# FFN output product of an encoder trunk: three pieces of Strassen's scheme and four tiles in the old form, in place of the direct product

## The chip, the cores and the metric

The kernel runs on one core of one Trainium2 chip, in one launch. The metric is the time of an execution in microseconds on the device; lower is better. Five engines of the core matter here: TensorE (PE; its weight loads are listed as PEld), VectorE (DVE), ScalarE (ACT), GpSimd (POOL) and SyncE (SP), which issues the transfers.

## The reference

Four post-norm layers over x of 512 tokens by 1024 features in float32. The mixers of the layers are multi-head latent attention, retention, gated linear attention and latent attention again. After each mixer comes a dense FFN with 2816 hidden features, and both are added to alpha times x and normalised:

```python
def swiglu_ffn(x, w_in, w_out):
    gate, up = jnp.split(x @ w_in, 2, axis=-1)
    return (jax.nn.silu(gate) * up) @ w_out
# in each layer, twice:  x <- layer_norm(alpha * x + sublayer(x))
```

The change touches the last product alone: 512 x 2816 by 2816 x 1024, once in each of four layers.

## The kernel before

Every float32 product is made of three matmuls on operands that are split into a rounded part hi and a rest lo: hi by hi, hi by lo, lo by hi (`mm3`, L126 to L130). ScalarE makes hi by a cast (L102), VectorE makes lo by a subtraction (L103). Weights arrive by transfers from SP's queue into one of three raw buffers (`wraw`), and their parts go to one of six `whi` and six `wlo` (`wload` and `wsplit`, L106 to L121). For six weights after the end of each stage POOL makes lo instead of VectorE (`relieve`). Sums stand in six buffers of PSUM (`ps`); two more (`tp`) take transposes.

The x of the layer is held twice: `xt`, four token tiles of 128 x 1024 in float32, which the layers add to and normalise, and `xh`, `xl`, its transposed and split form.

The FFN (`ffn`, L298) goes over 22 tiles of 128 hidden features. The first three are computed in two halves of the tokens, while the end of the mixer's normalisation still runs. Each later one takes a gate and an up projection of 24 matmuls of 512 columns each. `evac` then applies silu on ScalarE (L305), multiplies on VectorE (L306), and splits the product into `bh` and `bl`, which stay in SBUF for all 22 tiles. After the last tile comes the output product, `out_proj` (L212): one half of the 1024 output features at a time, all 22 feature tiles, with four sums, one for each token tile. The second half, `out_tail`, keeps its last eight feature tiles back and finishes one token tile after another with them, so that accumulation into `xt` (`acc`, L182 or L184), statistics (L186), normalisation (`ln_finish`, L205 and L206) and the transposes of the next stage (`x_to_xT`, L158) of one token tile stand beside the matmuls of the next. A path for four or fewer feature tiles (`nf <= 4`), used by the mixers of retention and gated linear attention, loads all weights first and does both halves of a token tile behind each other.

The program is written in this order, and a list scheduler places the instructions of each engine at compile time by that order and by the free buffers. Each engine then runs its own queue strictly in order; across engines it waits on semaphores.

Of the kernel before, what the change touches and what calls it, by code (L numbers as in the profile page):

```python
# [9 lines left out]
F32 = mybir.dt.float32  # L10
F32R = mybir.dt.float32r
I32 = mybir.dt.int32
AF = mybir.ActivationFunctionType
ALU = mybir.AluOpType
AX = mybir.AxisListType

P = 128
# [3 lines left out]
KT = D // P  # L21
DEPTH = 4
ALPHA = (2.0 * DEPTH) ** 0.25
LN_EPS = 1e-5
RMS_EPS = 1e-6
F = 2816
NF = F // P
# [23 lines left out]
class Trunk:  # L51
# [25 lines left out]
    @contextmanager  # L77
    def phase(self, **tags):

        with self.tc.tile_pool(name="phase", bufs=1, reuse_waits="tile") as self.bp:  # L80
            self.tags = dict(tags, b=self.nb - sum(tags.values()))
            yield

    def b(self, shape=(P, 512), dt=F32, name="b", tag="b"):
# [210 lines left out]
            self.proj_tile(t, wk, n, evac)  # L295


    def ffn(self, l, out=None):  # L298
        nc = self.nc
        w_in, w_out = self.ins["ffn_w_in"][l], self.ins["ffn_w_out"][l]  # L300
        hs = []

        def evac(pg, pu):
            s = self.b()
            nc.scalar.activation(s, pg, AF.Silu)  # L305
            nc.vector.tensor_tensor(s, pu, s, op=ALU.mult)  # L306
            h = self.bpair()
            self.split(h[0], h[1], s)
            hs.append(h)

        nh = 3
        first = []
        for f in range(nh):
            wg = self.wcols(w_in, 0, KT, f * P, P)
            wu = self.wcols(w_in, 0, KT, F + f * P, P)
            first.append((wg, self.ps()))
            first.append((wu, self.ps()))
        for t0 in (0, 2):
            for n, (w2, ps) in enumerate(first):
                self.proj_f(w2, ps[:, t0 * P : (t0 + 2) * P], KT, lambda k: self.xm(k, t0, t0 + 2))  # L320
                if n % 2:
                    self.flush(2 + n // 2)
        for f in range(nh):
            evac(first[2 * f][1], first[2 * f + 1][1])
        rot = False
        for f in range(nh, NF):
            if f == nh + 1:
                rot = self.before(l + 1, nc.vector)
            if f == NF - 4 and rot:
                self.rope_sin()  # L330
            wg = self.wcols(w_in, 0, KT, f * P, P)
            pg = self.ps()
            self.proj_f(wg, pg, KT, self.xm)
            wu = self.wcols(w_in, 0, KT, F + f * P, P)
            pu = self.ps()
            self.proj_f(wu, pu, KT, self.xm)
            evac(pg, pu)
        self.ln_begin(l, 1)
        st = lambda f, t: (hs[f][0][:, t * P : (t + 1) * P], hs[f][1][:, t * P : (t + 1) * P])
        self.out_proj(st, w_out, NF, ALPHA, True, out)  # L340

    def load_x(self, x):

# [805 lines left out]
    def run(self, out):  # L1149
        self.load_x(self.ins["x"][0])  # L1150
        for i in range(DEPTH):
            self.mixer(i)
            with self.phase():
                self.ffn(i, out[0] if i == DEPTH - 1 else None)


# [38 lines left out]
```

## Time and profile before

| | us |
|---|---|
| median of three runs | 2637.41 (2634.27 to 2637.83) |
| the profiled execution, its own time | 2635.14 |
| its span, first to last instruction | 2633.3 |
| mean granted TensorE clock | 0.994 of full speed |

The rows come from that one execution. The time outside of the span is 1.8 us. In rows of the trace, a line with L is the line of the kernel, `out<-in` are the program's names of the tiles, and x is how many instructions a row holds.

### The profile page before, as it was taken

The page shows a single profiled execution, that of the slowest core. Times are in us where ns is not written, and L with a number is a line of the kernel's source. Part 1 is how long each engine was busy: PE and PEld are TensorE (multiplying, and loading weights), DVE is VectorE, ACT ScalarE, POOL GpSimd, SP SyncE. Part 2 cuts the span into 40 slices and gives each one's busy share as a digit, 9 for nine tenths or more (in the row PEclk, how much of TensorE's full clock was granted, in tenths as well). Part 3 has the DMA queues.
Part 4 walks back from the last instruction along what each step waited for, and adds up shares of the span by engine and source line. Part 5 has one row for each costly group of instructions (what it writes and reads, how often), then busy time and mean ns, then how long its engine had stood idle before and what let it go on. Part 6 is the DMA issues. An engine that isn't in the chain of part 4 may idle for free.

```text
span 2633.3 us, 32309 instructions
## 1 busy us (share of the span) xinstructions
PE 2578.4 (98%) x12996; PEld 2191.5 (83%) x12996; DVE 1416.0 (54%) x2484; ACT 905.5 (34%) x1381; POOL 220.6 (8%) x231
## 2 busy tenths in 40 slices
PE   7999999999999999999999999999999999999998
PEld 6888888887888888988888998888888788888886
DVE  6877433228755548333326888833335686633334
ACT  4652323213333332322213654322312564322221
POOL 3002000001110103000002011100002200100001
PEclk9999999999999999999999999999999999999999
DMA  4212433233223232333233212333322221333321
GB/s 144 73 41 68 128 96 96 96 96 88 77 76 95 89 92 83 103 98 97 96 95 95 76 61 65 109 96 96 96 96 77 70 74 46 100 96 97 99 93 56
DMA packets 294711, 232.35 MB, mean 88 GB/s; under 512 B 21120, under 2 KB 244480, under 8 KB 294560
## 3 DMA queue, kind: packets, MB, share of 16 engines
q1 hardware_dynamic: 294560, 230.28, 28.8%
q8 instruction: 102, 1.67, 0.3%
q14 instruction: 49, 0.40, 0.0%
HBM read 228.15 MB, written 2.10 MB: 87 GB/s over the span
## 4 chain that ended last, share of the span: by engine, by line
PE 85%; DVE 9%; POOL 2%; issue 2%; ACT 2%; DMA 1%; DVEq 0%; SPq 0%; ACTq 0%; POOLq 0%
PE ps L128 27%; PE ps L130 27%; PE ps L129 27%; DVE xt L205 2%; DVE xt L206 1%; PE tp L557 1%; DVE lnst L186 1%; DVE xl L103 1%; PE ps L538 1%; DVE lnu L145 1%; PE ps L537 1%; DMA wraw<-in_mla_w_down 0%; DVE xt L184 0%; PE tp L158 0%; DVE bl L103 0%
## 5 line engine op out<-in xcount | busy, mean ns | idle before, releaser
L102 ACT CAST whi<-wraw 128x1024 fp32r<-128x1024 f32 (+3 forms) x414 | 431.0, 1042 | 1122.3 <-PE ps L130 379.4
L103 DVE TENSOR_TENSOR wlo<-wraw,whi 128x1024 fp32r<-128x1024 f32 (+2 forms) x366 | 444.1, 1215 | 660.4 <-ACT whi L102 647.8
L129 PE MATMUL ps<-xl,whi 128*128 128x512 f32 (+1 forms) x1792 | 659.9, 368 | 7.9 <-DVE xl L103 7.9
L128 PE MATMUL ps<-xh,whi 128*128 128x512 f32 (+1 forms) x1792 | 660.3, 368 | 0.0
L130 PE MATMUL ps<-xh,wlo 128*128 128x512 f32 (+1 forms) x1792 | 659.4, 368 | 0.0
L129 PEld LDWEIGHTS ps<-xl,whi 128*128 128x128 f32 x1792 | 341.2, 190 | 63.1 <-DVE xl L103 8.7
L128 PEld LDWEIGHTS ps<-xh,whi 128*128 128x128 f32 x1792 | 341.2, 190 | 54.9 <-issue 0.4
L130 PEld LDWEIGHTS ps<-xh,wlo 128*128 128x128 f32 x1792 | 341.0, 190 | 55.1
L128 PE MATMUL ps<-whi,bh 128*128 128x512 f32 (+1 forms) x960 | 368.7, 384 | 0.2 <-ACT bh L102 0.2
L130 PE MATMUL ps<-whi,bl 128*128 128x512 f32 (+1 forms) x960 | 367.2, 383 | 0.0
L129 PE MATMUL ps<-wlo,bh 128*128 128x512 f32 (+1 forms) x960 | 367.0, 382 | 0.0
L130 PE MATMUL ps<-whi,xl 128*128 128x512 f32 (+3 forms) x752 | 262.9, 350 | 5.2 <-DVE xl L103 5.2
L128 PE MATMUL ps<-whi,xh 128*128 128x512 f32 (+3 forms) x752 | 264.9, 352 | 1.1 <-ACT xh L102 1.1
L129 PE MATMUL ps<-wlo,xh 128*128 128x512 f32 (+3 forms) x752 | 262.1, 349 | 0.1
L103 POOL TENSOR_TENSOR wlo<-wraw,whi 128x1024 fp32r<-128x1024 f32 (+4 forms) x48 | 118.8, 2490 | 1649.1 <-ACT whi L102 1637.0
L130 PEld LDWEIGHTS ps<-whi,bl 128*128 128x128 f32 x960 | 180.5, 188 | 35.5 <-DVE bl L103 0.5
L128 PEld LDWEIGHTS ps<-whi,bh 128*128 128x128 f32 x960 | 180.5, 188 | 35.0 <-ACT bh L102 0.8
L129 PEld LDWEIGHTS ps<-wlo,bh 128*128 128x128 f32 x960 | 180.5, 188 | 34.7
L306 DVE TENSOR_TENSOR b<-ps,b 128x512 f32<-128x512 f32 x88 | 60.8, 691 | 262.1 <-PE ps L130 261.4
L130 PEld LDWEIGHTS ps<-whi,xl 128*128 128x128 f32 x752 | 142.8, 190 | 23.3 <-DVE xl L103 6.4
L128 PEld LDWEIGHTS ps<-whi,xh 128*128 128x128 f32 x752 | 143.2, 190 | 18.7 <-ACT xh L102 1.5
L129 PEld LDWEIGHTS ps<-wlo,xh 128*128 128x128 f32 x752 | 143.0, 190 | 17.3 <-POOL wlo L103 0.5
(220 smaller groups left out, 2772.6 us busy)
## 6 DMA issues: line engine op xcount, KB each, us to landing
wraw<-in_ffn_w_in SPq DMA_DIRECT2D x176, 512.0 KB, 3.8
wraw<-in_ffn_w_out SPq DMA_DIRECT2D x88, 512.0 KB, 3.3
wraw<-in_ret_w_in SPq DMA_DIRECT2D x48, 512.0 KB, 3.8
wraw<-in_gla_w_in SPq DMA_DIRECT2D x22, 512.0 KB, 3.5
wraw<-in_mla_w_o SPq DMA_DIRECT2D x16, 512.0 KB, 3.9
wraw<-in_ret_w_o SPq DMA_DIRECT2D x16, 512.0 KB, 4.7
wraw<-in_mla_w_down SPq DMA_DIRECT2D x8, 512.0 KB, 4.4
wraw<-in_mla_w_ukv SPq DMA_DIRECT2D x8, 512.0 KB, 3.7
```

What stands on the lines that cost most here:

```text
L102: a = self.nc.scalar.copy(hi, src)
L103: b = (eng or self.nc.vector).tensor_tensor(lo, src, hi.bitcast(F32), op=ALU.subtract)
L128: mm(out, s[0], m[0], start=start, stop=False)
L129: mm(out, s[0], m[1], start=False, stop=False)
L130: mm(out, s[1], m[0], start=False, stop=stop)
L145: stt(u, y, y, x, op0=ALU.mult, op1=ALU.mult)
L186: nc.vector.bn_stats(self.stats[t][:, half * 6 : half * 6 + 6], x)
L205: nc.vector.scalar_tensor_tensor(x[:, sl], x[:, sl], mv[:, 0:1], self.g[:, sl], op0=ALU.subtract, op1=ALU.mult)
L206: nc.vector.scalar_tensor_tensor(x[:, sl], x[:, sl], r, self.bb[:, sl], op0=ALU.mult, op1=ALU.add)
L306: nc.vector.tensor_tensor(s, pu, s, op=ALU.mult)
L537: nc.tensor.matmul(ps, qr[:, sl], krh, start=False, stop=False)
L538: nc.tensor.matmul(ps, qr[:, sl], krz[e], start=False, stop=True)
```

## The change

The 22 feature tiles of the output product are divided. Tiles 0 to 17 make nine pairs, and three pairs make a piece. For a piece, the four blocks are: tokens in two halves (two token tiles each), the pair's two members as the two halves of the inner dimension, and the output features in two halves. Seven products of sums and differences of blocks replace the eight block products; a product takes two token tiles x three pairs x three matmuls = 18, so a piece takes 126 in place of 144. A layer has 3 x 126 = 378 for tiles 0 to 17 in place of 432, and 96 for the last four tiles as before: 474 for 528. The program's order has 12782 instructions on PE in place of 12998, 2738 on DVE (2486), 1395 on ACT (1287), 540 on POOL (236) and 514 on SP (490).

Around the products:
- `evac` writes silu(gate) x up of tiles 0 to 17 into a buffer of seven blocks of 256 columns (`ft`, L325). At each second tile POOL makes the sums and differences of the blocks with four operations (L328 to L331), and one split of 7 x 256 = 1792 columns gives `fh` and `fl`.
- `ffn_out` loads four blocks of the weights, each in two parts (1024 and 512 columns: two pairs and one), makes the four sums and differences on POOL in place (L396), and splits all seven factors.
- The results are added into `xt` by `acc`. The products a11 and s2 are common to several blocks of the result: they are gathered in `u` by a copy on ScalarE (L417 or L420) and an add on POOL (L421), and after the third piece six adds on POOL bring `u` into `xt` (L450).
- The pieces stand behind tiles 7, 13 and 21 in the program. Behind the third comes `out_proj` with the last four tiles, which takes the path for four or fewer.

```diff
@@ -295,18 +295,52 @@
             self.proj_tile(t, wk, n, evac)
 
 
+
     def ffn(self, l, out=None):
         nc = self.nc
         w_in, w_out = self.ins["ffn_w_in"][l], self.ins["ffn_w_out"][l]
-        hs = []
-
-        def evac(pg, pu):
+        ns, pairs = 18, 3
+        self.fact, hs = {}, {}
+        self.u = self.b((P, 2, 512), tag="u", name="u")
+        half = lambda a: a.rearrange("p (a n) -> p a n", a=2)
+
+        def evac(f, pg, pu):
             s = self.b()
             nc.scalar.activation(s, pg, AF.Silu)
-            nc.vector.tensor_tensor(s, pu, s, op=ALU.mult)
-            h = self.bpair()
-            self.split(h[0], h[1], s)
-            hs.append(h)
+            if f >= ns:
+                if f < NF - 2:
+                    if f % 2 == 0:
+                        self.hp = self.b((P, 2, 512), F32R, "hh", "fh"), self.b((P, 2, 512), F32R, "hl", "fh")
+                    h = tuple(x[:, f % 2, :] for x in self.hp)
+                else:
+                    h = self.bpair()
+                nc.vector.tensor_tensor(s, pu, s, op=ALU.mult)
+                self.split(h[0], h[1], s)
+                hs[f] = h
+                return
+            if f % 2 == 0:
+                self.ft = self.b((P, 7, 256), tag="ft", name="ft")
+            ft = self.ft
+
+            nc.vector.tensor_tensor(ft[:, 2:4, :] if f % 2 else ft[:, 1::-1, :], half(pu), half(s), op=ALU.mult)
+            if f % 2:
+                tt = nc.gpsimd.tensor_tensor
+                tt(ft[:, 4, :], ft[:, 0, :], ft[:, 3, :], op=ALU.add)
+                tt(ft[:, 5, :], ft[:, 4, :], ft[:, 1, :], op=ALU.subtract)
+                tt(ft[:, 0, :], ft[:, 1, :], ft[:, 0, :], op=ALU.subtract)
+                tt(ft[:, 6, :], ft[:, 2, :], ft[:, 5, :], op=ALU.subtract)
+                h = self.b((P, 7, 256), F32R, "fh", "fh"), self.b((P, 7, 256), F32R, "fl", "fh")
+                self.split(h[0], h[1], ft)
+                self.fact[f // 2] = h
+
+        def in_f(f):
+            wg = self.wcols(w_in, 0, KT, f * P, P)
+            pg = self.ps()
+            self.proj_f(wg, pg, KT, self.xm)
+            wu = self.wcols(w_in, 0, KT, F + f * P, P)
+            pu = self.ps()
+            self.proj_f(wu, pu, KT, self.xm)
+            evac(f, pg, pu)
 
...
@@ -321,23 +355,99 @@
                 if n % 2:
                     self.flush(2 + n // 2)
         for f in range(nh):
-            evac(first[2 * f][1], first[2 * f + 1][1])
+            evac(f, first[2 * f][1], first[2 * f + 1][1])
         rot = False
         for f in range(nh, NF):
             if f == nh + 1:
                 rot = self.before(l + 1, nc.vector)
             if f == NF - 4 and rot:
                 self.rope_sin()
-            wg = self.wcols(w_in, 0, KT, f * P, P)
-            pg = self.ps()
-            self.proj_f(wg, pg, KT, self.xm)
-            wu = self.wcols(w_in, 0, KT, F + f * P, P)
-            pu = self.ps()
-            self.proj_f(wu, pu, KT, self.xm)
-            evac(pg, pu)
+            in_f(f)
+
+            c = {7: 0, 13: 1, NF - 1: 2}.get(f)
+            if c is not None:
+                self.ffn_out(w_out, c * pairs, pairs, c == 0, c == 2)
         self.ln_begin(l, 1)
-        st = lambda f, t: (hs[f][0][:, t * P : (t + 1) * P], hs[f][1][:, t * P : (t + 1) * P])
-        self.out_proj(st, w_out, NF, ALPHA, True, out)
+        st = lambda f, t: tuple(x[:, t * P : (t + 1) * P] for x in hs[ns + f])
+        self.out_proj(st, w_out[ns * P :], NF - ns, None, True, out)
+
+    def ffn_out(self, w, g0, n, begin, end):
+
+        nc = self.nc
+        rows = w[2 * g0 * P : 2 * (g0 + n) * P, :].rearrange("(g a p) c -> a p g c", a=2, p=P)
+        parts = [(0, 2), (2, n)]
+        blocks = {}
+
+        def load(name, a, c):
+            for j, (i0, i1) in enumerate(parts):
+                if i1 - i0 == 1:
+                    t = self.b((P, 1, 512), name="wb")
+                elif name == "1":
+                    t = self.wp.tile([P, 2, 512], F32, tag="wraw", name="wraw", bufs=self.nraw)
+                else:
+                    t = self.b((P, 2, 512), name="wt", tag="t")
+                nc.sync.dma_start(t, rows[a][:, i0:i1, c * 512 : c * 512 + 512])
+                blocks[name, j] = t
+
+        def sub(to, x, y):
+
+            for j in range(2):
+                o = blocks[to, j]
+                nc.gpsimd.tensor_tensor(o, blocks[x, j], blocks[y, j], op=ALU.subtract)
+
+        def parted(name):
+            res = []
+            for j, (i0, i1) in enumerate(parts):
+                hi, lo = self.wsplit(blocks[name, j], i1 - i0, 512)
+                res += [(hi[:, i, :], lo[:, i, :]) for i in range(i1 - i0)]
+            return res
+
+        def product(slot, wk, to, u=None):
+
+            ps = [self.ps() for _ in range(2)]
+            for tt in range(2):
+                for i in range(n):
+                    s2 = tuple(x[:, slot, tt * P : (tt + 1) * P] for x in self.fact[g0 + i])
+                    self.mm3(ps[tt], s2, wk[i], i == 0, i == n - 1)
+                for hf, c, first in to:
+                    self.acc(2 * hf + tt, c, ps[tt], ALPHA if first else None, False)
+                if u is not None:
+                    x = self.u[:, tt, :]
+                    if u:
+                        nc.scalar.copy(x, ps[tt])
+                    else:
+                        m = self.b()
+                        nc.scalar.copy(m, ps[tt])
+                        nc.gpsimd.tensor_tensor(x, x, m, op=ALU.add)
+
+        s3, a11, a12, a22, s1, s2, s4 = range(7)
+        load("1", 0, 0)
+        w11 = parted("1")
+        load("2", 0, 1)
+        sub("1", "2", "1")
+        t1 = parted("1")
+        load("3", 1, 1)
+        sub("1", "3", "1")
+        t2 = parted("1")
+        sub("2", "3", "2")
+        load("4", 1, 0)
+        product(a11, w11, [(0, 0, begin)], begin)
+        product(s1, t1, [(0, 1, begin), (1, 1, begin)])
+        w21 = parted("4")
+        sub("4", "4", "1")
+        product(s2, t2, [], False)
+        w22 = parted("3")
+        product(a12, w21, [(0, 0, False)])
+        t3 = parted("2")
+        product(s4, w22, [(0, 1, False)])
+        t4 = parted("4")
+        product(s3, t3, [(1, 0, begin), (1, 1, False)])
+        product(a22, t4, [(1, 0, False)])
+        if end:
+            for tt in range(2):
+                for hf, c in ((0, 1), (1, 0), (1, 1)):
+                    x = self.xt[2 * hf + tt][:, c * 512 : c * 512 + 512]
+                    nc.gpsimd.tensor_tensor(x, x, self.u[:, tt, :], op=ALU.add)
 
...
@@ -1150,7 +1260,7 @@
         self.load_x(self.ins["x"][0])
         for i in range(DEPTH):
             self.mixer(i)
-            with self.phase():
+            with self.phase(fh=8, ft=1, t=3, u=1, b=10):
                 self.ffn(i, out[0] if i == DEPTH - 1 else None)
```

Three places where the order of the queues differs. First VectorE's queue around the seventh and eighth feature tile. Before, each tile's product (`b`, L306) and its split alternate with the splits of weights:

```order
L306 TENSOR_TENSOR b_3215<-ps_3190,b_3215 128x512
L103 TENSOR_TENSOR wlo_3394<-wraw_3391,whi_3393 128x1024
L103 TENSOR_TENSOR bl_3219<-b_3215,bh_3218 128x512
L103 TENSOR_TENSOR wlo_3432<-wraw_3429,whi_3431 128x1024
L306 TENSOR_TENSOR b_3284<-ps_3259,b_3284 128x512
L103 TENSOR_TENSOR wlo_3463<-wraw_3460,whi_3462 128x1024
L103 TENSOR_TENSOR bl_3288<-b_3284,bh_3287 128x512
```

Now the first piece begins there: `wb` and `wraw` are its weight blocks in two parts, `wt` the block of product a12, `ft` the factors of the pair of tiles 6 and 7, and `xt0` to `xt3` the sums.

```order
L103 TENSOR_TENSOR wlo_3319<-wb_3298,whi_3318 128x512
L325 TENSOR_TENSOR ft_3221<-ps_3260,b_3285 128x512
L103 TENSOR_TENSOR wlo_3329<-wraw_3296,whi_3328 128x1024
L103 TENSOR_TENSOR wlo_3333<-wb_3298,whi_3332 128x512
L184 SCALAR_TENSOR_TENSOR xt0_80<-xt0_80,ps_3342 128x512
L103 TENSOR_TENSOR fl_3293<-ft_3221,fh_3292 128x1792
L184 SCALAR_TENSOR_TENSOR xt1_81<-xt1_81,ps_3343 128x512
L184 SCALAR_TENSOR_TENSOR xt0_80<-xt0_80,ps_3366 128x512
L184 SCALAR_TENSOR_TENSOR xt2_82<-xt2_82,ps_3366 128x512
L184 SCALAR_TENSOR_TENSOR xt1_81<-xt1_81,ps_3367 128x512
L184 SCALAR_TENSOR_TENSOR xt3_83<-xt3_83,ps_3367 128x512
L103 TENSOR_TENSOR wlo_3391<-wt_3338,whi_3390 128x1024
```

The low part of the factors (`fl`) and five accumulations stand ahead of the weight of a12 (`wlo_3391`). On ScalarE, at the same place (`b_3219` and `b_3285` are silu of tiles 6 and 7, `whi_3304` is the second part of a11's weight, `whi_3390` a12's):

```order
L309 ACTIVATE b_3219<-ps_3163 128x512
L309 ACTIVATE b_3285<-ps_3229 128x512
L102 CAST whi_3304<-wb_3298 128x512
L102 CAST whi_3314<-wraw_3296 128x1024
L102 CAST whi_3318<-wb_3298 128x512
L102 CAST whi_3328<-wraw_3296 128x1024
L102 CAST whi_3332<-wb_3298 128x512
L102 CAST fh_3292<-ft_3221 128x1792
L102 CAST whi_3390<-wt_3338 128x1024
```

The silu of the eighth tile stands ahead of the cast of a11's second part. POOL, which has no row of this kind in the stretch before, now has:

```order
L396 TENSOR_TENSOR wb_3298<-wb_3310,wb_3298 128x512
L396 TENSOR_TENSOR wb_3310<-wb_3324,wb_3310 128x512
L396 TENSOR_TENSOR wraw_3296<-wt_3322,wraw_3296 128x1024
L396 TENSOR_TENSOR wb_3298<-wb_3324,wb_3298 128x512
L328 TENSOR_TENSOR ft_3221<-ft_3221 128x256
L329 TENSOR_TENSOR ft_3221<-ft_3221 128x256
L330 TENSOR_TENSOR ft_3221<-ft_3221 128x256
L331 TENSOR_TENSOR ft_3221<-ft_3221 128x256
L421 TENSOR_TENSOR u_2533<-u_2533,b_3411 128x512
L396 TENSOR_TENSOR wt_3338<-wt_3338,wraw_3296 128x1024
```

The four operations on factors stand behind four subtractions of weights. The third place is the last piece on VectorE, behind the product and split of tile 21 (`b_4752`):

```order
L317 TENSOR_TENSOR b_4752<-ps_4727,b_4752 128x512
L103 TENSOR_TENSOR bl_4755<-b_4752,bh_4754 128x512
L103 TENSOR_TENSOR wlo_4768<-wb_4761,whi_4767 128x512
L103 TENSOR_TENSOR wlo_4778<-wraw_4759,whi_4777 128x1024
L103 TENSOR_TENSOR wlo_4782<-wb_4761,whi_4781 128x512
L182 TENSOR_TENSOR xt0_80<-ps_4805,xt0_80 128x512
L182 TENSOR_TENSOR xt1_81<-ps_4806,xt1_81 128x512
L182 TENSOR_TENSOR xt0_80<-ps_4833,xt0_80 128x512
L103 TENSOR_TENSOR wlo_4792<-wraw_4759,whi_4791 128x1024
```

Here the second part of a11's weight (`wlo_4768`) follows tile 21's split directly, and no factors of a pair stand between.

## Rows read from the trace of the kernel before

**Rows 1.** Part 1 of the page: busy us, share of the span, instructions.

```profile
PE 2578.4 (98%) x12996; PEld 2191.5 (83%) x12996; DVE 1416.0 (54%) x2484; ACT 905.5 (34%) x1381; POOL 220.6 (8%) x231
```

**Rows 2.** Part 4 of the page: the chain that ended last, by engine.

```profile
PE 85%; DVE 9%; POOL 2%; issue 2%; ACT 2%; DMA 1%; DVEq 0%; SPq 0%; ACTq 0%; POOLq 0%
```

**Rows 3.** Windows of the first FFN: its projections, then its output product.

```profile
core 0: us, PE busy (x) PEld busy (x) DVE busy (x) ACT busy (x) POOL busy (x), PEclk, DMA share, GB/s
300.00:440.00 140.00, 140.00 (x620) 115.95 (x619) 48.66 (x52) 40.91 (x52) 0.00 (x0) 1.00 0.33 97
440.00:585.00 145.00, 145.00 (x641) 120.10 (x640) 41.93 (x43) 34.10 (x38) 2.40 (x1) 1.00 0.30 98
```

**Rows 4.** Timeline of PE: first and last of 117 rows in a row.

```profile
439.71 0.39 PE L128 MATMUL ps<-xh,whi 128*128 128x512 f32 x1
...
466.00 0.39 PE L130 MATMUL ps<-xh,wlo 128*128 128x512 f32 x1
```

**Rows 5.** Groups by line and form (busy, mean ns | idle); last: one tile's view.

```profile
L102 ACT CAST whi<-wraw 128x1024 fp32r<-128x1024 f32 x397 | 418.3, 1054 | 1104.4 <-issue 371.8 <-PE ps L130 370.1 <-PE ps L129 314.2
L102 ACT CAST bh<-b 128x512 fp32r<-128x512 f32 x148 | 91.8, 621 | 57.6 <-DVE b L679 20.8 <-DVE b L753 19.0 <-DVE b L1024 11.1
L305 ACT ACTIVATE b<-ps 128x512 f32<-128x512 f32 x88 | 51.8, 588 | 0.0
L103 DVE TENSOR_TENSOR wlo<-wraw,whi 128x1024 fp32r<-128x1024 f32 x355 | 435.6, 1228 | 652.5 <-ACT whi L102 640.1
L103 DVE TENSOR_TENSOR bl<-b,bh 128x512 fp32r<-128x512 f32 x148 | 101.3, 685 | 12.3 <-ACT bh L102 12.0
L306 DVE TENSOR_TENSOR b<-ps,b 128x512 f32<-128x512 f32 x88 | 60.8, 691 | 262.1 <-PE ps L130 261.4 <-ACT b L305 0.7
L182 DVE TENSOR_TENSOR xt<-ps,xt 128x512 f32<-128x512 f32 x32 | 21.5, 683 | 8.9 <-PE ps L130 8.9
L793 POOL TENSOR_TENSOR b<-b 128x512 f32<-128x512 f32 x16 | 21.3, 1334 | 1.3
L103 POOL TENSOR_TENSOR wlo<-wraw,whi 128x576 fp32r<-128x576 f32 x1 | 1.4, 1450 | 0.0
...
L103 POOL TENSOR_TENSOR wlo<-wraw,whi x48: 1450/2405/2876, 209.7 to 2259.8; 128x1024 fp32r<-128x1024 f32 x42, 128x864 fp32r<-128x864 f32 x2, 128x960 fp32r<-128x960 f32 x2, 128x576 fp32r<-128x576 f32 x1
```

**Rows 6.** Timeline of POOL in retention: start, us, operation.

```profile
705.87 1.29 POOL L792 TENSOR_TENSOR b<-b 128x512 f32<-128x512 f32 x1 [1.53 <-DVE gnb L789]
...
708.83 2.28 POOL L792 TENSOR_TENSOR b<-b 128x512 f32<-128x512 f32 x1
711.19 1.62 POOL L793 TENSOR_TENSOR b<-b 128x512 f32<-128x512 f32 x1
```

**Rows 7.** Timeline of DVE in the same stretch.

```profile
708.23 1.72 DVE L103 TENSOR_TENSOR wlo<-wraw,whi 128x1024 fp32r<-128x1024 f32 x1
709.87 0.68 DVE L678 TENSOR_TENSOR b<-ps,tab 128x512 f32<-128x512 f32 x1
...
711.58 2.31 DVE L103 TENSOR_TENSOR wlo<-wraw,whi 128x1024 fp32r<-128x1024 f32 x1
```

**Rows 8.** Windows: two stops of PE, each with the stretch behind it.

```profile
619.40:623.50 4.10, 0.42 (x2) 0.00 (x0) 3.96 (x9) 0.59 (x1) 1.64 (x2) 1.00 0.00 0
623.50:626.90 3.40, 3.33 (x8) 2.67 (x9) 1.21 (x3) 0.00 (x0) 0.00 (x0) 0.50 0.00 0
238.90:241.20 2.30, 0.17 (x2) 0.00 (x0) 2.30 (x3) 0.00 (x0) 2.30 (x2) 1.00 0.78 225
241.20:244.60 3.40, 3.30 (x15) 3.30 (x16) 3.40 (x4) 1.05 (x1) 3.36 (x2) 0.50 0.61 176
```

**Rows 9.** PE's waits by line: 585 to 640 us, then 1039 to 1060 us.

```profile
PE ps L130 <- DVE xl L103: 3.7, 1, 3.7
PE ps L129 <- DVE xl L103: 3.4, 1, 3.4
```

**Rows 10.** Part 6 of the page: transfers, KB each, us from issue to landing.

```profile
wraw<-in_ffn_w_out SPq DMA_DIRECT2D x88, 512.0 KB, 3.3
```

More of the change, by code (lines that the diff above doesn't have):

```diff
@@ L80, in phase @@
         with self.tc.tile_pool(name="phase", bufs=1, reuse_waits="tile") as self.bp:
-            self.tags = dict(tags, b=self.nb - sum(tags.values()))
+            self.tags = {"b": self.nb - sum(tags.values()), **tags}
             yield
```

## The prediction

> **What bounds the kernel now.** I read the busy shares first: TensorE is busy for 2578.4 of 2633.3 us, VectorE for 1416.0, ScalarE for 905.5, POOL for 220.6 [rows 1]. The chain that ended last runs 85% over TensorE [rows 2]. Shares are means over stages, so I cut the FFN of layer 0 out: in its projections TensorE is busy for all 140.00 us, in its output product for all of 145.00, at granted clock 1.00, while VectorE is busy for 48.66 and 41.93 us, ScalarE for 40.91 and 34.10, POOL for 0.00 and 2.40 [rows 3]. So here only TensorE's work counts, and whatever leaves it comes off the end, as long as the operands come in time. The distance of one matmul to the next: from 439.71 to 466.00 us there are 117 rows of 128x512, hence 26.29/116 = 0.2266 us each [rows 4].
>
> **What is removed.** 54 matmuls of 528 in each of four layers, 216 x 0.2266 = 49.0 us. This is the whole gain; there is no wait to take away, since TensorE has none there. A piece has seven products of 18 matmuls, 4.08 us each, 28.6 us in all, and there are three pieces in a layer.
>
> **What is added.** Work for the other engines, most of it at the piece's start. Durations [rows 5]: a ScalarE cast of 512 elements 0.62 us, of 1024 1.05, silu 0.59; VectorE's low part of 512 0.69, of 1024 1.23, the product with the PSUM input 0.69, an accumulation 0.68. A factor split has 1792 elements: continued by the slope between 512 and 1024, my estimates are 1.70 on ScalarE and 2.04 on VectorE. POOL takes 1.33 for 512 (1.29 at best [rows 6], I take 1.30), 1.45 for 576 and 2.40 for 1024; for its adds of 256 I estimate 0.75 by the same line. Summed over a layer there is ample room: 21 weights of 1536 elements for 18 of 1024, nine factor splits, 48 accumulations more; VectorE was idle for two thirds of the time. So only where they stand in line counts.
>
> One more thing prices them. When POOL and VectorE both work on operands in SBUF, one waits for the other: at 708.23 VectorE's split of 1024 holds until 709.95, POOL's product, issued at 708.83, takes 2.28 us instead of 1.3; POOL's next, from 711.19 to 712.81, makes VectorE's split of 711.58 take 2.31 us instead of 1.23 [rows 6, 7]. VectorE's operations on PSUM (709.87, 0.68 us) go through unhindered [rows 7]. I therefore let POOL and VectorE take turns wherever both have only SBUF inputs.
>
> The Trainium skill ("Advanced Engine Details and Errata", VectorE Performance Modes) speaks of VectorE's two-port instructions as those that block POOL, and a tensor_tensor on fp32 is in none of the modes it lists with two ports; by that alone there would be no turns here and the time would be rival N's, below. Another page ("SBUF — State Buffer", SBUF: two separate sides) also counts a VectorE operation with two SBUF inputs against a POOL operation that reads SBUF; by that the sum below holds, and the rows at 708 to 714 us agree, 2.31 us for 1.23.
>
> **First and second piece (eight in all).** T = 0 is the end of tile f7's second projection, when product a11 starts. s1 starts at 4.08, s2 at 8.16, a12 at 12.24, and a12's second matmul wants the low part of its weight at 12.47. I follow the order of the queues to it.
> - ScalarE: silu of f7's gate from -5.2 (the gate's sum ends at -5.4) to -4.6. The cast of a11's second part stands behind it: ready at -4.0; VectorE's low part at -3.3.
> - Only then POOL may subtract in the same buffer (s1's second part): -3.2 to -1.9. With turns: VectorE's split of s1's first part to -0.65, POOL's next subtraction of 512 to 0.65, VectorE's split of 512 to 1.35, POOL's of 1024 to 3.8 and of 512 to 5.15, VectorE's of 1024 to 6.4, POOL's first add of 256 to 7.15, VectorE's of 512 to 7.85, POOL's other three to 10.1.
> - These four adds make f7's factors, and all of that split stands ahead of a12's weight: ScalarE's cast of 1792 from 10.15 to 11.9, VectorE's low part from 11.95 to 14.0.
> - Behind it in VectorE's queue stand five accumulations of products long done, 5 x 0.69, to 17.45. POOL has started an add on u (17.15 to 18.45), and a12's low part follows, 18.45 to 19.7.
>
> It is wanted at 12.47: TensorE stands for 7.2 us. After a stop the clock is granted at half: after those of 4.1 and of 2.3 us, 3.40 us at 0.50 [rows 8], in which 8 full matmuls went at 0.427 us, so 8 x 0.20 = 1.6 us more. Together 8.8 us for each piece. What is late behind a12 (s4, s3) gains the same 7 us and is not late again. Lower bound: without turns the chain gives the last POOL add at 6.2, the factors' low part at 10.0, five accumulations to 13.5 and the low part at 14.8: 2.3 us stop, 1.6 of half clock, 3.9. Upper: a second stop at s4 with its own half clock, 12.
>
> **Last piece (four in all).** Here f17's factors are long done, but f21's product with PSUM and split (0.2 to 2.2) come first; then a split and a POOL subtraction by turns. The low parts come at 2.95, 5.6, 7.6, 12.65, 17.25, 19.25, 22.95, 24.95 and 27.5. In TensorE's order, without stops, they would be wanted at matmul 14, 20, 26, 37, 55, 61, 73, 79 and 91, that is 3.2, 4.5, 5.9, 8.4, 12.5, 13.8, 16.5, 17.9 and 20.6. The lateness grows by pieces of 0.7 to 2.5 us to 27.5 - 20.6 = 6.9; I take 7.0, without half clock since most stops are short. Bounds: 2.5 without turns, 10 with half clock.
>
> **The tail.** The last four tiles run token tile by token tile, with both halves' accumulation and statistics in each; VectorE gets some 1.4 us more per token tile (two operations of 0.68), and the six adds of u on POOL come before. The waits behind the old tails are 3.7 us after an FFN, and 3.4 after retention, which has the form that the FFN gets [rows 9]. I take +1 us over four layers, bounds -3 and +12. The weights' transfers: 3.3 us to land [rows 10], issued tens of us ahead, DMA share 0.30 [rows 3]; nothing.
>
> **The sum**, against the profiled execution (2635.1): -49.0 + 8 x 8.8 + 4 x 7.0 + 1 = +50.4, 2685.5. The median of the runs lies 2.3 above the profiled one: 2688.
>
> **Rivals.**
> - N, no turns, or a shorter chain: 2635.1 - 49.0 + 8 x 3.9 + 4 x 2.5 + 1 = 2628.3, 2631 by the median. For it: the rows on turns are few, all from a stage with other operations, and the 256 adds are estimates. Against it: the two rows at 708 and 711 us fit to 0.1 us. 0.18.
> - G, the gain comes whole: all waits hidden, 2587, 2589 by the median. It needs a12's weight 7 us earlier than the queue gives it, for instance by factor adds of 0.3 us and accumulations out of the way. The FFN's idle VectorE [rows 3] speaks for it, the order of the queue against it. 0.07. This and N are the rivals on the other side; the point from which they decide is a stop of about 2.6 us or less at a12 (2.6 + 1.6 = 4.2 us, 8 x 4.2 + 4 x 3.6 = 48).
> - W, each stop gives two stretches of half clock, and the tails cost: 12 for the early pieces, 10 for the last: 2635.1 - 49.0 + 96 + 40 + 1 = 2723, 2725 by the median. 0.09.
> - M, the forecast, 2688, its own range 2650 to 2715 (stops at a12 of 4 to 9 us): 0.66.
>
> **Numbers.** Changes below 0.2%, 5 us, can't be told from none. Faster (under 2632): G, and of N 0.10: 0.17. Within: 0.05 of N. Slower: M, W and the rest of N: 0.78. The range leaves out G and the ends of N and W: 2620 to 2722.
>
> **What would show it.** TensorE's waits should have one of some 7 us at a12's second matmul, for the low part of the weight, eight times; the granted clock 0.50 behind it; VectorE's splits ahead of it stretched to 2 us and more while POOL works; in the last piece some nine waits of 0.7 to 2.5 us. TensorE's busy time should fall by 49 us less what half clock adds (8 x 1.6). It is wrong if the low part comes by 13 us after a11's start, if POOL's adds of 256 take much less than 0.75 us, if VectorE's splits keep their 1.23 us beside POOL, or if the tails' waits behind the layer norm grow from 4 us to 8.

## The result and the profile after

The changed kernel takes 2676.39 us (median of four runs, 2675.07 to 2679.52), the kernel before 2637.62: a ratio of 1.0151, with an interval of 1.0133 to 1.0169. The change costs 38.8 us. The profiled execution was the slowest of the four (2679.52); it has a span of 2677.7 us and a mean granted clock of 0.983.

The busy shares of the page after, to be read against [rows 1]:

```profile
PE 2565.8 (96%) x12780; PEld 2164.6 (81%) x12780; DVE 1733.0 (65%) x2736; ACT 1005.8 (38%) x1489; POOL 667.4 (25%) x535
```

TensorE has 216 matmuls less, worth 49.0 us, and the span is 44 us longer. So more than 90 us in which TensorE newly stands or runs slower have to be found. TensorE's waits in the kernel after, with us in total, times, and the longest:

```profile
PE ps L129 <- DVE wlo L103: 41.9, 27, 3.8
PE tp L158 <- DVE xt L206: 21.2, 9, 5.8
```

The first row is new: low parts of weights that come late inside the pieces and at the last four tiles. The second, the transposes behind the normalisation, was smaller in the kernel before:

```profile
PE tp L158 <- DVE xt L206: 5.4, 2, 3.6
```

The first piece of the first FFN, in three windows with the columns of [rows 3]; then that piece as a whole, and the last piece of the same FFN:

```profile
335.60:347.90 12.30, 12.30 (x56) 10.17 (x55) 6.37 (x7) 5.32 (x6) 8.46 (x7) 1.00 0.00 0
347.90:351.90 4.00, 0.40 (x2) 0.00 (x0) 4.00 (x7) 3.34 (x5) 0.73 (x1) 1.00 0.00 0
351.90:356.00 4.10, 3.89 (x11) 3.01 (x12) 4.10 (x3) 1.15 (x3) 4.10 (x3) 0.64 0.00 0
```

```profile
335.60:369.90 34.30, 30.49 (x128) 24.66 (x127) 28.37 (x29) 14.45 (x18) 17.20 (x11) 0.95 0.24 76
556.50:589.90 33.40, 30.69 (x128) 23.13 (x127) 30.61 (x28) 15.46 (x21) 22.75 (x12) 1.00 0.08 25
```

The products a11, s1 and s2 run without a stop for 12.3 us. Then TensorE stands for 4.0 us at a12's second matmul, and 4.1 us at a mean clock of 0.64 follow. 126 matmuls take 28.55 us at the pitch of [rows 4]; the two pieces take 34.3 and 33.4 us, so one loses 5.7 us and the other 4.8. The other layers repeat it (one of the eight early pieces loses 7.0). Summed over the twelve pieces that is 66.7 us, 47.0 in the eight early ones and 19.7 in the four last ones. Then 38.8 + 49.0 - 66.7 leaves about 21 us for the tails (27 us if the 44.4 us between the two profiled spans are taken in place of the medians' 38.8).

VectorE in the first piece (start, us, operation; a11 starts at 335.67):

```profile
332.51 2.20 DVE L103 TENSOR_TENSOR wlo<-wraw,whi 128x1024 fp32r<-128x1024 f32 x1 [0.25 <-ACT whi L102]
334.64 1.77 DVE L103 TENSOR_TENSOR wlo<-wb,whi 128x512 fp32r<-128x512 f32 x1
336.33 0.68 DVE L325 TENSOR_TENSOR ft<-ps,b 128x512 f32<-128x512 f32 x1
339.78 1.23 DVE L103 TENSOR_TENSOR wlo<-wraw,whi 128x1024 fp32r<-128x1024 f32 x1 [2.77 <-ACT whi L102]
340.93 1.22 DVE L103 TENSOR_TENSOR wlo<-wb,whi 128x512 fp32r<-128x512 f32 x1
342.07 0.67 DVE L184 SCALAR_TENSOR_TENSOR xt<-xt,ps 128x512 f32<-128x512 f32 x1
345.90 2.03 DVE L103 TENSOR_TENSOR fl<-ft,fh 128x1792 fp32r<-128x1792 f32 x1 [3.16 <-ACT fh L102]
347.85 3.07 DVE L184 SCALAR_TENSOR_TENSOR xt<-xt,ps 128x512 f32<-128x512 f32 x5
350.84 1.22 DVE L103 TENSOR_TENSOR wlo<-wt,whi 128x1024 fp32r<-128x1024 f32 x1
```

POOL beside it:

```profile
332.34 3.52 POOL L396 TENSOR_TENSOR wb<-wb 128x512 f32<-128x512 f32 x2 [13.70 <-DVE wlo L103]
335.83 2.84 POOL L396 TENSOR_TENSOR wraw<-wt,wraw 128x1024 f32<-128x1024 f32 x1
338.62 1.30 POOL L396 TENSOR_TENSOR wb<-wb 128x512 f32<-128x512 f32 x1
339.88 1.73 POOL L328 TENSOR_TENSOR ft<-ft 128x256 f32<-128x256 f32 x1
...
343.42 0.73 POOL L331 TENSOR_TENSOR ft<-ft 128x256 f32<-128x256 f32 x1
351.17 2.03 POOL L421 TENSOR_TENSOR u<-u,b 128x512 f32<-128x512 f32 x1 [7.03 <-ACT b L420]
```

The chain is the one that was forecast, in its order: weights' subtractions, factor operations, factor split (ScalarE's cast ends at 345.88), five accumulations, a12's low part, which ends at 352.06 and is wanted at 348.14. The split of 1024 at 332.51 takes 2.20 us beside POOL, the operation with a PSUM input at 336.33 takes 0.68 beside POOL's subtraction of 335.83.

In the last piece of that layer a11 starts at 556.58. The low parts of s2's first part, a12's first part and s4's second part:

```profile
567.04 1.23 DVE L103 TENSOR_TENSOR wlo<-wraw,whi 128x1024 fp32r<-128x1024 f32 x1 [1.57 <-ACT whi L102]
...
570.58 1.80 DVE L103 TENSOR_TENSOR wlo<-wt,whi 128x1024 fp32r<-128x1024 f32 x1
...
577.34 1.78 DVE L103 TENSOR_TENSOR wlo<-wb,whi 128x512 fp32r<-128x512 f32 x1
```

### The profile page after: what moved, and what is told of

Read it like the earlier page. It is cut to its first block, busy times and chain, and to the rows that moved or that the text cites. A ratio compares the mean times of both kernels' runs of the same rounds, so it can differ in the third digit from the quotient of the medians.

```text
span 2677.7 us, 32782 instructions
## 1 busy us (share of the span) xinstructions
PE 2565.8 (96%) x12780; PEld 2164.6 (81%) x12780; DVE 1733.0 (65%) x2736; ACT 1005.8 (38%) x1489; POOL 667.4 (25%) x535
## 4 chain that ended last, share of the span: by engine, by line
PE 71%; DVE 15%; issue 8%; POOL 3%; ACT 2%; DMA 1%; SPq 0%; DVEq 0%; POOLq 0%; ACTq 0%
PE ps L129 23%; PE ps L128 23%; PE ps L130 22%; DVE wlo L103 4%; DVE xt L182 2%; DVE xt L205 2%; DVE lnst L186 1%; DVE xt L206 1%; PE tp L667 1%; POOL wraw L396 1%; ACT whi L102 1%; DVE xt L184 1%; PE tp L158 1%; PE ps L648 1%; DVE xl L103 1%
## 5 line engine op out<-in xcount | busy, mean ns | idle before, releaser
L102 ACT CAST whi<-wraw 128x1024 fp32r<-128x1024 f32 (+2 forms) x378 | 391.2, 1040 | 662.4 <-PE ps L129 207.1
L103 DVE TENSOR_TENSOR wlo<-wraw,whi 128x1024 fp32r<-128x1024 f32 (+2 forms) x330 | 427.4, 1300 | 296.6 <-ACT whi L102 291.7
L129 PE MATMUL ps<-wlo,fh 128*128 128x512 f32 x504 | 206.0, 409 | 37.8 <-DVE wlo L103 37.4
L128 PE MATMUL ps<-whi,fh 128*128 128x512 f32 x504 | 201.2, 402 | 3.1 <-ACT whi L102 3.1
L130 PE MATMUL ps<-whi,fl 128*128 128x512 f32 x504 | 202.9, 403 | 0.0
L103 DVE TENSOR_TENSOR fl<-ft,fh 128x1792 fp32r<-128x1792 f32 x36 | 72.9, 2026 | 144.5 <-ACT fh L102 144.5
L328 POOL TENSOR_TENSOR ft<-ft 128x256 f32<-128x256 f32 x36 | 38.6, 1071 | 509.0 <-DVE ft L325 509.0
L129 PEld LDWEIGHTS ps<-wlo,fh 128*128 128x128 f32 x504 | 98.2, 195 | 70.9 <-DVE wlo L103 50.2
L182 DVE TENSOR_TENSOR xt<-ps,xt 128x512 f32<-128x512 f32 x224 | 145.8, 679 | 8.8 <-PE ps L130 8.8
```

The costliest lines, as they stand in the source:

```text
L102: a = self.nc.scalar.copy(hi, src)
L103: b = (eng or self.nc.vector).tensor_tensor(lo, src, hi.bitcast(F32), op=ALU.subtract)
L128: mm(out, s[0], m[0], start=start, stop=False)
L129: mm(out, s[0], m[1], start=False, stop=False)
L130: mm(out, s[1], m[0], start=False, stop=stop)
L182: nc.vector.tensor_tensor(x, ps, x, op=ALU.add)
```

## The experiments

The theory (Q): a12's weight is late because of its place on VectorE, behind the split of a pair's factors and behind accumulations, and the factors are late because POOL and VectorE take turns. Two rivals for the pieces:
- T: the weights' subtractions are late by themselves.
- N: turns cost nothing.

For the tail three causes stand against each other:
- F: the form with both halves in each token tile.
- U: POOL's adds of u.
- V: VectorE's rest of the piece.

Ratios are to runs of the kernel before on the same chip.

**Pieces one tile later.**

```diff
-            c = {7: 0, 13: 1, NF - 1: 2}.get(f)
+            c = {8: 0, 14: 1, NF - 2: 2}.get(f)
```

> The three pieces stand one feature tile later (behind tiles 8, 14 and 20): the split of the pair's factors is then done before a piece begins, and the rest is as in the changed kernel (2676 us). Theory Q (the stop of 4 us at a12's low part comes from the factor split and the five accumulations that stand ahead of it in VectorE's queue): the eight stops with their half clock vanish, 8 x 5.7 = 46 us, the last piece keeps its 4.9 us, 2625 to 2632. Rival T (the turns of POOL and VectorE over the weights' subtractions make the chain late by themselves): stops of 2 us and more stay at s2 or a12, 2645 to 2665. If the adds of u on POOL, which are now over before the last four tiles, were what slows the tail, another 10 us go.

2621.11 us, ratio 0.9943 (0.9927 to 0.996). VectorE in the first piece; a11 starts at 346.67, so a12's low part is wanted at 359.14:

```profile
353.49 1.27 DVE L184 SCALAR_TENSOR_TENSOR xt<-xt,ps 128x512 f32<-128x512 f32 x2
354.68 1.21 DVE L103 TENSOR_TENSOR wlo<-wt,whi 128x1024 fp32r<-128x1024 f32 x1
```

It ends at 355.89, three us early, and the eight early pieces lose nothing. The last pieces keep 4.8 to 5.1 us each. Rival T falls for the early pieces: the same subtractions in the same turns are in time as soon as no factor split stands there. The time is below the range of Q without U (2625 to 2632) and near the upper end of that with U (10 us less, 2615 to 2622). So part of the gain is the tail's, which had to be looked at apart.

**Factor operations on VectorE.**

```diff
-                tt = nc.gpsimd.tensor_tensor
+                tt = nc.vector.tensor_tensor
```

> The four factor operations of 256 columns run on VectorE in place of POOL; the places of the pieces are unchanged. With turns, VectorE's adds alternate with POOL's subtractions of weights: the factors' low part ends about 10.5 us after a11's start, a12's low part at 14.8 (wanted at 12.5), so stops of 2.3 us in place of 4.0 and 2660 to 2668 us. Without turns (rival N) the adds end by 3 us, the factors by 7, the low part by 11: no stop, 2628 to 2636.

2648.99 us, ratio 1.0047 (1.0032 to 1.0062): between the two ranges and in neither. VectorE, with a11's start at 335.21:

```profile
336.58 1.90 DVE L328 TENSOR_TENSOR ft<-ft 128x256 f32<-128x256 f32 x1
338.52 1.40 DVE L329 TENSOR_TENSOR ft<-ft 128x256 f32<-128x256 f32 x1
339.85 0.41 DVE L330 TENSOR_TENSOR ft<-ft 128x256 f32<-128x256 f32 x1
...
342.85 2.01 DVE L103 TENSOR_TENSOR fl<-ft,fh 128x1792 fp32r<-128x1792 f32 x1
344.79 3.07 DVE L184 SCALAR_TENSOR_TENSOR xt<-xt,ps 128x512 f32<-128x512 f32 x5
347.78 1.76 DVE L103 TENSOR_TENSOR wlo<-wt,whi 128x1024 fp32r<-128x1024 f32 x1
```

An operation that takes 0.41 us alone takes 1.90 and 1.40 beside POOL's subtractions: the turns are there, and N's time is missed by 13 us or more. a12's stop is 1.9 us in this piece (2.3 was expected), 1.9 to 2.1 in the eight. What was sized wrongly is the clock: after this stop it stays whole. So seven of the eight pieces lose 2.3 to 2.5 us and not the 4.0 that the expected range stands for (2.3 of stop and 1.7 of half clock); the eighth loses 3.9.

```profile
347.40:349.40 2.00, 0.44 (x2) 0.02 (x1) 2.00 (x2) 1.68 (x3) 1.05 (x1) 1.00 0.00 0
349.40:353.40 4.00, 3.81 (x17) 3.16 (x18) 4.00 (x4) 0.25 (x1) 3.72 (x2) 1.00 0.00 0
```

**Weights' subtractions on VectorE.**

```diff
-                nc.gpsimd.tensor_tensor(o, blocks[x, j], blocks[y, j], op=ALU.subtract)
+                nc.vector.tensor_tensor(o, blocks[x, j], blocks[y, j], op=ALU.subtract)
```

> The weights' sums and differences run on VectorE in place of POOL, the factors' four operations stay on POOL, the places of the pieces are those of the changed kernel. In the first two pieces the factor split now stands ahead of s2's low part. With turns, POOL's four operations alternate with VectorE's subtractions, the factors' low part ends 11.4 us after a11's start and s2's at 12.6 (wanted at 8.4): a stop of about 4 us at s2 in place of a12; the last piece has no turns in its chain and loses 2.5 to 3 us for 4.9: 2660 to 2676 us. Without turns the factors are done at 8, s2's low part at 9.4, a stop of 1 us: 2625 to 2635.

2670.12 us, ratio 1.0122 (1.0105 to 1.0139), in the range with turns. The stop moves to s2 as expected, but in parts: in the first piece 2.6 us at s2's first two matmuls, then 1.2 at a12 and 0.5 at s4. The early pieces lose 5.1 to 5.8 us, the last ones 3.5. Taking the weights from POOL doesn't help while the factor split has that place.

**Only the tail's form.** The kernel before, with tiles 0 to 17 as direct products and the last four by the path for four or fewer.

```diff
+        if last and nf > 8:
+            for half in halves:
...
+                for t in range(NT):
+                    self.acc(t, half, pss[t], coef, False)
+            self.out_proj(lambda f, t: st(nf - 4 + f, t), w[(nf - 4) * P :], 4, None, last, out)
+            return
```

> The kernel before (2637.5 us), without Strassen's scheme, but with its last four feature tiles in the form for four or fewer (both halves of a token tile behind each other), tiles 0 to 17 as direct products ahead of it. Theory F (this form, in which both halves' accumulation and statistics fall into each token tile, makes VectorE late in the tail): 15 to 25 us more than before, 2652 to 2662, with waits for xt L206 in the tails. Rival U (POOL's adds of u into xt, and their turns with VectorE, make the tail late): within 5 us of before.

2642.01 us against 2636.54, ratio 1.0023 (1.0014 to 1.0033): 5.5 us, just outside the rival's bound of 5 and far from F's 15 to 25. F is real and a quarter of what it had to be. TensorE's wait for the normalised tile is 12.3 us for the 5.4 of before, and 21.2 after the change:

```profile
PE tp L158 <- DVE xt L206: 12.3, 5, 5.3
```

**All three pieces late.** The third piece behind tile 18; tiles 18 and 19 are split together behind tile 19.

```diff
-            c = {7: 0, 13: 1, NF - 1: 2}.get(f)
+            c = {8: 0, 14: 1, 18: 2}.get(f)
...
+                nc.vector.tensor_tensor(self.ft[:, f % 2, :], pu, s, op=ALU.mult)
+                if f % 2:
+                    hp = self.b((P, 2, 512), F32R, "hh", "fh"), self.b((P, 2, 512), F32R, "hl", "fh")
+                    self.split(hp[0], hp[1], self.ft)
```

> As the run with the pieces one tile later, but the third piece behind tile 18, and tiles 18 and 19 split together behind tile 19, so that no cast of a product stands between silu and the cast of a11's second part on ScalarE. Theory Q: no stops in any piece, 66.7 us less than the changed kernel, 2605 to 2612; if POOL's adds of u were what slows the tail (theory U), 2590 to 2600, since they are over three tiles before it. Rival T: stops of 2 us or more stay in each piece, 2635 or more.

2599.42 us, ratio 0.9859 (0.9844 to 0.9873). The three pieces of the first layer, in windows:

```profile
346.30:374.90 28.60, 28.60 (x127) 23.68 (x127) 25.31 (x29) 13.89 (x19) 13.19 (x7) 1.00 0.32 101
440.10:468.70 28.60, 28.60 (x128) 23.70 (x127) 25.27 (x26) 13.59 (x18) 17.74 (x9) 1.00 0.27 82
512.20:540.80 28.60, 28.60 (x128) 23.70 (x127) 25.84 (x25) 13.05 (x17) 21.30 (x11) 1.00 0.07 20
```

TensorE works through all three, and so it does in the other layers. VectorE is busy for 25 of 28.6 us there; an FFN whose VectorE was idle for two thirds has a stretch with a tenth to spare. The time is at the upper end of the range of Q with U.

**Without the adds of u.** The last loop of `ffn_out` (L446 to L450) is taken out.

> The changed kernel without its last step: POOL's six additions of u into xt behind the third piece are left out, so the sums of a11 and s2 are missing in three blocks of the result. All else is unchanged, VectorE's accumulations and weight splits of the piece too. Theory U (the additions and their turns with VectorE make the tail late): 10 to 17 us less than the changed kernel, 2660 to 2667, and the tail of the first layer loses 5 us for 9.5. Rival V (VectorE is late with the piece's own splits and accumulations, which stand ahead of the last four tiles in its queue): at most 5 us less, 2671 to 2677.

2667.74 us, ratio 1.0112 (1.0096 to 1.0127): 8.7 us below the changed kernel. Between U's 10 and V's 5, nearer to U. The pieces lose what they lost; the two waits for weights at the first layer's last four tiles (0.8 and 0.7 us in the changed kernel) are gone, and one wait for the normalisation is halved (2.1 to 0.9 us). The cause is again the turns, now with the weights that VectorE splits for the last four tiles. In the changed kernel:

```profile
585.02 3.86 POOL L450 TENSOR_TENSOR xt<-xt,u 128x512 f32<-128x512 f32 x2 [4.76 <-DVE xt L182]
586.00 3.96 DVE L103 TENSOR_TENSOR wlo<-wraw,whi 128x1024 fp32r<-128x1024 f32 x2
...
591.31 5.76 POOL L450 TENSOR_TENSOR xt<-xt,u 128x512 f32<-128x512 f32 x3 [2.42 <-DVE xt L182]
```

Without the adds:

```profile
586.08 2.34 DVE L103 TENSOR_TENSOR wlo<-wraw,whi 128x1024 fp32r<-128x1024 f32 x2
```

**The first token tile in another order.** Pieces as in the run with all three late; in the FFN's last product the first token tile takes tiles 18 to 20 of both halves before tile 21.

```diff
...
+                if lag and t == 0:
+                    todo.sort(key=lambda x: x[1] == nf - 1)
...
```

> As the run with all pieces late (2599.4 us), and in the last four tiles' product of the FFN the first token tile takes tiles 18 to 20 of both halves before tile 21, whose split is late by 1.6 us there. Theory: the waits for tile 21's low part vanish in the two or three layers that have it, 3 to 6 us less, 2593 to 2597. Rival: VectorE, which is late in the tail anyway, hands the time back at the normalisation: 2598 to 2601.

2594.82 us, ratio 0.984 (0.9825 to 0.9855), in the range: 42.9 us of the 49.0 are kept, and the rest is about F's 5.5. TensorE's wait for the normalised tile is 12.6 us in all, where the tail's form alone has 12.3. This version is faster than both kernels.

**a12's split ahead of s1 in the program.**

```diff
         product(a11, w11, [(0, 0, begin)], begin)
-        product(s1, t1, [(0, 1, begin), (1, 1, begin)])
         w21 = parted("4")
+        product(s1, t1, [(0, 1, begin), (1, 1, begin)])
```

> The split of a12's weight stands ahead of product s1 in the program, with the pieces where the changed kernel has them: four of the five accumulations then follow it on VectorE, the factor split still stands ahead. Theory Q, with the durations of the changed kernel's trace: the factors' low part ends 12.3 us after a11's start, one accumulation to 12.9, a12's low part 14.1 for 16.4: stops of 1.6 us for 4.0, 2 us lost for 5.7, 2644 to 2652 us. Rival (a12's low part waits for its own cast or for POOL, not for its place on VectorE): no change, 2672 to 2680.

2656.27 us, ratio 1.0071 (1.0056 to 1.0086): 20 us less than the changed kernel, where 24 to 32 were expected. a12's stop is 1.57 us in the first piece, as forecast (1.6), but s4 now stops for 1.0. The second piece of each layer stops for 2.05 at a12; the first pieces lose 3.2 us and the second ones 4.7, where 2 was forecast. In the first piece:

```profile
347.98 0.68 DVE L184 SCALAR_TENSOR_TENSOR xt<-xt,ps 128x512 f32<-128x512 f32 x1
348.58 1.22 DVE L103 TENSOR_TENSOR wlo<-wt,whi 128x1024 fp32r<-128x1024 f32 x1
349.71 0.68 DVE L103 TENSOR_TENSOR wlo<-wb,whi 128x512 fp32r<-128x512 f32 x1
350.31 2.47 DVE L184 SCALAR_TENSOR_TENSOR xt<-xt,ps 128x512 f32<-128x512 f32 x4
352.71 2.30 DVE L103 TENSOR_TENSOR wlo<-wt,whi 128x1024 fp32r<-128x1024 f32 x1
```

The four accumulations only move one weight on, and that weight's split meets a turn of POOL (2.30 for 1.23 us). What the stop at a12 had hidden is late next.

**Without the factor split at the pieces' start.** For tiles 7 and 13 the four operations and the split are left out.

```diff
-            if f % 2:
+            if f in (7, 13):
+                self.fact[f // 2] = self.fact[f // 2 - 1]
+            elif f % 2:
                 tt = nc.gpsimd.tensor_tensor
```

> The changed kernel without the four factor operations and the factor split of tiles 7 and 13 (the sixth and seventh pair's values take their place, so the results of two pairs are wrong); all other pairs keep theirs, the pieces stay behind tiles 7, 13 and 21. Theory Q: nothing but accumulations stands ahead of a12's low part, which comes at 10.5 us after a11's start or sooner, and the eight stops vanish: 46 us less, 2627 to 2634. Rival T (the weights' subtractions in turns with VectorE are late by themselves): stops of 1 us and more stay, 2640 or more.

2627.11 us, ratio 0.9958 (0.9941 to 0.9975), just at the lower end of Q's range: the early pieces lose nothing, with all weights' subtractions and accumulations in their place. So the pair's factor work, the four operations and the split together, is the cause of the eight stops, shown from both sides (moved away, and left out). The accumulations behind it add to a stop, as the run before this one shows, but make none by themselves.

## Why the prediction was right, and where its sum was off

- **The gain** of 49.0 us: right. Where nothing stops it, a piece's 126 matmuls take 28.6 us, as reckoned. With the stops away (2594.82), 42.9 us are seen, and the missing 6 are about what the tail's form costs alone (5.5).
- **The chain in front of a12**: right in each link, and eight times. Its end was forecast at 19.7 us after a11's start and is 352.06 - 335.67 = 16.4; wanted at 12.47 both times. Three terms make the 3.3 us: the last factor operation is done at 8.5 and not at 10.1, 0.9 of it since POOL finished with the weights at 4.25 and not at 5.15; five accumulations run in 3.07 us and not 3.45, since they follow each other more closely than their single durations; and POOL's add on u, which I let go ahead of a12's split (1.3 us), starts behind it. So the stop was 4.0 us and not 7.2, at the lower end of the 4 to 9 that the forecast gave itself, and the eight pieces lose 47.0 us and not 8 x 8.8 = 70.4.
- **Half clock**: right in size for these stops (1.7 us lost for 1.6). In the piece that loses 7.0 the granted clock is 0.50 for 6.8 us, from 1261.00 to 1267.80: rival W's case, once in eight. TensorE's busy time, which I named as a sign, fell by 12.6 us and not by 36: it also holds the matmuls of the last pieces, which run late one by one (30.69 us busy in a piece of 28.55), and of the tails; it is no clean measure of what was removed.
- **The turns**: right. In the trace after, no split of 1024 columns that is free of POOL's two-input operations takes more than 1.23 us (269 of them), and of the 98 that one overlaps the longest takes 3.42. Of the two runs that move POOL's work to VectorE, one lies in the range with turns; the other lies between the ranges, but with a stop that there would not be without turns. The note in the Trainium skill ("Advanced Engine Details and Errata", VectorE Performance Modes) names two-port instructions alone; by it there would have been no turns, rival N. The Trainium skill's page "SBUF — State Buffer" (SBUF: two separate sides) also counts two SBUF inputs, and the 1.90 us for an operation of 0.41 agree.
- **The last piece**: the mechanism is right, 4.8 to 5.1 us for 7.0. The lateness does grow from weight to weight, but the chain is shorter than reckoned: counted from a11's start, the three low parts shown above come at 11.7, 15.8 and 22.5, where 12.65, 17.25 and 24.95 were forecast. The greatest lateness is 22.5 - 17.9 = 4.6. It shows as three waits of 0.9 to 1.0 us, one of 0.5 and some of 0.2, not as nine of 0.7 to 2.5.
- **The tail**: this term failed. "I take +1 us over four layers, bounds -3 and +12" was 21. I counted the two VectorE operations for each token tile and set POOL's adds of u down as done before. They are not: two start at 585.02 and three more at 591.31, beside the splits for the last four tiles, and the turns that I had priced in the pieces I left out here. Of the 21 us the form alone is 5.5, the adds of u 8.7. The remaining 7 are open: with the third piece three tiles earlier 11.9 of the 49.0 us are still missing (2599.42), and they shrink to 6.1 only when the first token tile also waits less for tile 21 (2594.82). That points at the nearness of piece and tail, rival V, but no run takes its operations apart. The sign set for the tail, waits growing from 4 us to 8, was not quite reached: in the first tail the waits behind the normalisation grow from 3.7 to 6.4 us.

The two errors have opposite signs, -32 us in the pieces (66.7 for 98.4) and +20 in the tail (21 for 1). That the sum lies 12 us off and not 32 is luck.

That this is a matter of places, not of work, is the strongest finding: the factors whose split stops TensorE are those of tiles 6 and 7, and piece one uses tiles 0 to 5 only. Nobody needs them until the second piece, 87 us after their split (435.24 against 347.93). The forecast followed the chain through them and didn't say so; had it, it would have named the cheap way out.

## What to carry to other kernels

Price the work that a saving hands to other engines at the place where their queues hold it, not by their mean idle time: with an engine idle for two thirds, 5 us of a factor split and accumulations ahead of one urgent weight cost 47 us in eight places, nearly the whole saving of 49. Start a stage that needs prepared operands where no large preparation for something else has just entered the queues (here one tile later: 55 us, 47 of them the eight stops), and let what is needed much later stand behind what is needed now. And look at the tail of a stage as a queue of its own: what is written right ahead of it, on any engine, can come into its latency (here six adds on POOL: 8.7 us).

## What the runs showed of the hardware

POOL and VectorE exclude each other operation by operation where both have only SBUF inputs: 0.41 us became 1.90, 0.69 became 1.77, 1.23 became 2.20. VectorE's operations with one PSUM input are not held up: 0.68 us beside POOL's subtraction at 336.33, and 0.67 to 0.69 in all 114 two-input operations of 512 float32 columns in the trace after that POOL's overlap.

The length of a stop of TensorE alone doesn't tell whether the granted clock falls. A stop of 4.0 us was followed by a mean of 0.64 over 4.1 us (whole clock at first, then half: 0.52 from 352.90 to 356.40), one of 1.9 us by the whole clock (factor operations on VectorE), one of 2.3 us in the kernel before by 0.50 [rows 8]. In the run with the factor operations on VectorE four pieces have the same stop of 2.1 us at a12, and only behind one of them did the clock fall (0.69 from 1249.50 to 1255.00, but 1.00 from 446.00 to 451.00).
